# Two-layer mixer and expert model on one core: residual gain in half rows, last two tiles combined by TensorE in both layers

## The chip, the cores and the metric

One core of a Trainium2 chip runs the whole program. The metric is the device time of one execution in microseconds (us), median of three. The engines are named as the profile names them: PE is TensorE (matmuls), DVE VectorE, ACT ScalarE, POOL GpSimd, SP SyncE, which issues most DMAs.

## What is computed

512 tokens of width 1024 pass through two layers and then a second block (a gated delta rule beside a linear recurrence, and an MLP). Of the two layers, cut to what matters here:

```python
for l in range(2):
    p = x @ w_in[l]                                   # input projection
    heads = concat(_mla(p...), _mlstm(p...), _ssd(p...))
    mix = heads @ w_out[l]                            # out projection
    x = layernorm(sqrt2 * x + mix, ln1_g[l], ln1_b[l])
    ffn = hier_moe(x, ...)                            # 16 experts, 2 per token, weighted sum
    x = layernorm(sqrt2 * x + ffn, ln2_g[l], ln2_b[l])
return second_block(x, ...)
```

All of it is float32. A product keeps full precision by splitting each operand into a high and a low part (fp32r) and adding three matmuls: high x high (L124), high x low (L125), low x high (L126).

## The kernel before, in words

The 512 tokens are four tiles of 128 rows (NT = 4). The program's text isn't the order that runs: a scheduler orders the instructions of each engine, and each engine then works through its own list, waiting where data isn't there. `layer(l)` holds what the change touches:

- **Out projection.** `R` holds the residual (4 tiles x 1024). In layer 1 it is the last layer's output without gain and bias, so `ln2_g` and `ln2_b` are loaded into two `Ye` tiles and applied to whole rows: L2065 (multiply) and L2066 (add), tiles 1 and 3 on POOL, 0 and 2 on DVE. Then `fin` (L2084 on) adds each 128x256 quarter of the product to `R` (L2086), which frees the product's PSUM buffer `mm`.
- **Experts.** Twenty steps of a loop run 16 experts, each in stages. `expert` gathers its rows, multiplies by the gate and up weights (`pg`, `py`), forms `ehh` (L1118), transposes it (L1123), multiplies by the down weight, copies the two halves of the result from PSUM into a `Ye` tile (ACT, L1133), and SP stores that to `Yd` in DRAM (L2124). `self.last` remembers `ehh` of the last expert.
- **Gate.** After the loop `self.gate` is `self.last`: POOL copies one element of it into the buffer of the next weight load (L219), so that SP can issue that load (`w_gates` in layer 0, `w_in` of the second block in layer 1) only when the element exists.
- **Overflow.** A branch (L2155) handles experts with too many tokens. Ahead of it SP waits for the outstanding transfers, the last store to `Yd` among them.
- **Combine.** POOL gathers, for each tile, the rows of its two experts (L2168) into two buffers (`GTl`, `G`, `GTh`, or halves of `raw`). A tile is added to `R` either by DVE, two scalar_tensor_tensor of 128x1024 (L2174, L2175), or by PE with diagonal matrices `dg` of the routing weights (L2182) and DVE adding the 512-wide halves (L2183). Before, layer 0 does all four tiles by DVE, layer 1 tiles 2 and 3 by PE.
- **Norm.** `moments` takes the mean, the squares on ACT (L483) and the inverse root in six small operations (L165, L166), in layer 0 on POOL for tiles 0 and 1. In layer 0 ACT normalises (L2189), PE transposes (L378), and `to_T` evicts the eight transposed 128x128 blocks into `GTh` with gain and bias, columns 3, 6, 7 on ACT (L393), the rest on DVE (L395). ACT casts the high parts (`actTh`), and POOL (tiles 0 to 2) or DVE (tile 3) subtracts the low parts (`actTl`, L139). The next layer's products of that tile (`mm`, 24 matmuls of 312 columns) need both.

Of the kernel before, what the change touches and what calls it, by code (L numbers as in the profile page):

```python
# [11 lines left out]
AF = mybir.ActivationFunctionType  # L12
OP = mybir.AluOpType
AX = mybir.AxisListType

P = 128
S = 512
NT = S // P
D = 1024
# [51 lines left out]
class Kernel:  # L71
# [297 lines left out]
    def to_T(self, dst, src, i, gc=None, bc=None, pool=None, rs=None):  # L369


        nc = self.nc
        for g in range(KD // 4):
            p = self.ps("tr", [P, 4, P])
            for j in range(4):
                f = 4 * g + j
                if rs is None:
                    nc.tensor.transpose(p[:, j, :], src[:, f * P:(f + 1) * P], self.ident)  # L378
                else:
                    nc.tensor.matmul(p[:, j, :], src[:, f * P:(f + 1) * P], rs, start=True, stop=True)  # L380
            d = dst[:, 4 * g:4 * g + 4, i * P:(i + 1) * P]
            if gc is None:
                self.split(d, p)
                continue
            y = None if bc is None else self.t(pool, "GTh", [P, KD, P], bufs=2)[:, 0:4]
            for j in range(4):
                f = 4 * g + j
                if bc is None:
                    nc.scalar.activation(d.h[:, j], p[:, j], AF.Copy, scale=gc[:, f:f + 1])
                    nc.vector.scalar_tensor_tensor(d.l[:, j], p[:, j], gc[:, f:f + 1], d.h[:, j], op0=OP.mult,  # L390
                                                   op1=OP.subtract)
                elif f in (3, 6, 7):
                    nc.scalar.activation(y[:, j], p[:, j], AF.Identity, scale=gc[:, f:f + 1], bias=bc[:, f:f + 1])  # L393
                else:
                    nc.vector.tensor_scalar(y[:, j], p[:, j], gc[:, f:f + 1], bc[:, f:f + 1], op0=OP.mult, op1=OP.add)  # L395
            if bc is not None:
                self.split(d, y, "act", "pool" if i < 3 else "dve")


    def proj_tok(self, xT, key, ncols, evac, kd=KD, ks=None):  # L400
# [691 lines left out]
    def expert(self, pool, parts, idx, store, n=CAP):  # L1092


        nc, v = self.nc, self.nc.vector
        G = self.t(pool, "G", [P, D], bufs=4)
        self.rows.append(G)
        nc.gpsimd.indirect_dma_start(out=G[:n], out_offset=None, in_=self.Xd,  # L1098
                                     in_offset=bass.IndirectOffsetOnAxis(ap=idx[:n], axis=0))
        yield  # L1100
        GT = self.hl(pool, "GT", [P, KD, P], bufs=2)[:, :, 0:n]
        for g in range(2):
            p = self.ps("tr", [P, 4, n])
            for j in range(4):
                nc.tensor.transpose(p[:, j, :], G[:n, 4 * g + j:D:KD], self.ident[:n, :n])
            self.split(GT[:, 4 * g:4 * g + 4, :], p)
        yield
        self.turn = not self.turn
        pg = self.ps("pg" if self.turn else "py", [n, 512])
        for q in range(2):  # L1110
            with parts[q] as w:
                for k in range(KD):
                    self.mm(pg[:, q * 256:(q + 1) * 256], GT[:, k, :], w[k], start=k == 0, stop=k == KD - 1)
        th = self.t(pool, "eth", [P, 256], bufs=2)[:n]
        nc.scalar.activation(th, pg[:, 0:256], AF.Tanh, scale=0.5)
        v.scalar_tensor_tensor(th, th, 1.0, pg[:, 0:256], op0=OP.add, op1=OP.mult)
        hh = self.t(pool, "ehh", [P, 2, P], bufs=2)[:n]
        v.scalar_tensor_tensor(hh.rearrange("t f p -> t p f"), th.rearrange("t (p f) -> t p f", f=2), 0.5,  # L1118
                               pg[:, 256:512].rearrange("t (p f) -> t p f", f=2), op0=OP.mult, op1=OP.mult)
        self.last = hh[:, 0, :]  # L1120
        pt = self.ps("ht", [P, 2, n])
        for f in range(2):
            nc.tensor.transpose(pt[:, f, :], hh[:, f, :], self.ident[:n, :n])  # L1123
        hT = self.hl(pool, "hT", [P, 2, P], bufs=2)[:, :, 0:n]
        self.split(hT, pt)
        yield
        Y = self.t(pool, "Ye", [P, D], bufs=2)[:n]
        with parts[2] as w:
            for z in range(2):
                py = self.ps("mm", [n, 512])  # L1130
                for f in range(2):
                    self.mm(py, hT[:, f, :], w[f][:, z * 512:(z + 1) * 512], start=f == 0, stop=f == 1)
                nc.scalar.copy(Y[:, z * 512:(z + 1) * 512], py)  # L1133
        store(Y)
        yield
# [911 lines left out]
    def layer(self, l):  # L2047
# [4 lines left out]
        with ExitStack() as c:  # L2052
# [5 lines left out]
            if l:  # L2058

                gb = [self.t(mo, "Ye", [P, D], bufs=2) for _ in range(2)]  # L2060
                for t, n in zip(gb, ("ln2_g", "ln2_b")):
                    self.bcast_load(t, a[n][l - 1], D)
                for i in (1, 0, 2, 3):
                    e = nc.gpsimd if i % 2 else v
                    e.tensor_tensor(R[:, i], R[:, i], gb[0], op=OP.mult)  # L2065
                    e.tensor_tensor(R[:, i], R[:, i], gb[1], op=OP.add)  # L2066

            halves = lambda: self.t(mo, "raw", [P, 2 * UNIT]).rearrange("p (z d) -> p z d", z=2)
            gb = halves()
# [13 lines left out]

            def fin(i, q, p):  # L2084
                r = R[:, i, q * 256:(q + 1) * 256]
                v.scalar_tensor_tensor(r, r, 2 ** 0.5, p, op0=OP.mult, op1=OP.add, accum_out=sums[:, i, q:q + 1])  # L2086
                if q == 1 and i == 0:
                    self.router_fold(mo, rw, bias, gc)
                if q < 3:
                    return  # L2090
                xt = self.t(mo, "Ye", [P, D], bufs=2)
                for g in range(2):
                    p = self.ps("tr", [P, 4 * P])
                    for j in range(4):
                        f = 4 * g + j
                        nc.tensor.transpose(p[:, j * P:(j + 1) * P], R[:, i, f * P:(f + 1) * P], self.ident)
                    (nc.vector.tensor_copy if g else nc.scalar.copy)(xt[:, g * 512:(g + 1) * 512], p)
                r = R[:, i]
                nm, rs = self.moments(mo, r, sums[:, i], self.t(mo, "G", [P, D], bufs=4), 1e-5)
                u = self.t(mo, "G", [P, D], bufs=4)  # L2100
                v.scalar_tensor_tensor(u, r, nm, gb[0], op0=OP.add, op1=OP.mult)
                for k in range(KD):
                    nc.tensor.matmul(pl[:, i, :], xt[:, k * P:(k + 1) * P], rw[:, k], start=k == 0, stop=k == KD - 1)
                v.scalar_tensor_tensor(LG[:, i], pl[:, i], rs, bias, op0=OP.mult, op1=OP.add)
                v.scalar_tensor_tensor(r, u, rs, gb[1], op0=OP.mult, op1=OP.add)
                self.dump(f"x1_{l}", r, i)
                nc.sync.dma_start(self.Xd[tok(i), :], r)
# [10 lines left out]
            n = nc.values_load(cnt[0:1, 0:1], min_val=0, max_val=S)  # L2118

            ex = {}  # L2120
            if l:

                dg = self.t(mo, "dg", [P, 2, NT, P])
            store = lambda e: lambda y: nc.sync.dma_start(self.Yd[e * CAP:e * CAP + CAP, :], y)  # L2124
            for s in range(16 + 4):
                if s == 8 and l == 0:
# [2 lines left out]
                    self.pat = [("act", "dve")]  # L2129
                if s == 1:  # L2130
                    self.params(l + 1)
                if l and 4 <= s < 12:
                    j, i = divmod(s - 4, NT)
                    nc.scalar.activation(dg[:, j, i], self.ident, AF.Copy, scale=wts[j][:, i:i + 1])

                if s < 16:
                    idx = self.slot_ids(mo, PM[:, s, :], 0, "idx")
# [23 lines left out]
            Yg = [self.t(mo, tag, [P, D], bufs=n) for tag, n in [("GTl", 2)] * 2 + [("G", 4)] * 4 + [("GTh", 2)] * 2 * l]  # L2161
            if l == 0:
                z = halves()
                Yg += [z[:, 0], z[:, 1]]
            Yg = [Yg[2 * i:2 * i + 2] for i in range(NT)]
            for i in range(NT):
                for j in range(2):
# [2 lines left out]
            self.gate = [Yg[3][0]] * 2  # L2170
            for i in range(NT):
                r = R[:, i]
                if l == 0 or i < 2:
                    v.scalar_tensor_tensor(r, Yg[i][0], wts[0][:, i:i + 1], r, op0=OP.mult, op1=OP.add)  # L2174
                    v.scalar_tensor_tensor(r, Yg[i][1], wts[1][:, i:i + 1], r, op0=OP.mult, op1=OP.add,  # L2175
                                           accum_out=sums[:, i, 0:1])
                else:
                    for hf in range(2):
                        py = self.ps(("pg", "py")[hf], [P, 512])
                        hs = slice(hf * 512, (hf + 1) * 512)  # L2180
                        for j in range(2):
                            nc.tensor.matmul(py, dg[:, j, i], Yg[i][j][:, hs], start=j == 0, stop=j == 1)  # L2182
                        v.scalar_tensor_tensor(r[:, hs], py, 1.0, r[:, hs], op0=OP.mult, op1=OP.add,  # L2183
                                               accum_out=sums[:, i, hf:hf + 1])
                nm, rs = self.moments(mo, r, sums[:, i, 0:1 if l == 0 or i < 2 else 2], Yg[i][0], 0.5e-5, nc.gpsimd if i < 2 and l == 0 else v)
                xh = Yg[i][1]
                if l == 0:
                    v.tensor_tensor(nm, nm, rs, op=OP.mult)
# [75 lines left out]
```

## Time and profile before

| | us |
|---|---|
| three runs | 1707.49, 1707.58, 1709.02 |
| median | 1707.58 |
| the profiled execution's own time | 1710.83 |
| its span, first to last instruction | 1709.0 |
| PE busy | 1569.1 (92%) |
| DVE / ACT / POOL busy | 1274.3 / 835.7 / 513.2 |
| mean granted TensorE clock | 0.956 of full |

A profile shows one execution. Rows of a timeline begin with a start time and a duration in us; in square brackets stands how long the engine was idle before, and what ended that. "x2" means two instructions in one row. Times in the text are on that time line.

### The profile page before, as it was taken

The numbers are of one execution on the slowest core, as the hardware profiler recorded it, in microseconds if no ns is written. First come the engines' busy times: TensorE is split into PE (matmuls) and PEld (weight loads), VectorE is DVE, ScalarE is ACT, GpSimd is POOL, SyncE is SP. The second block draws the span as 40 slices with busy tenths as digits, with TensorE's granted clock in tenths as the row PEclk, the third lists the DMA queues.
The fourth block names the chain that finished last, engine by engine and source line by source line (L and its number), as shares of the span: only waits on it lengthen the run. The fifth ranks groups of instructions, "written<-read, shape, count | busy, mean of one in ns | idle before, by whom it ended". The sixth has DMA issues, their size and how long they took to land. (4 is left out here: it accounts for less than half of the span.)

```text
span 1709.0 us, 29588 instructions
## 1 busy us (share of the span) xinstructions
PE 1569.1 (92%) x11563; PEld 1402.5 (82%) x11563; DVE 1274.3 (75%) x2466; ACT 835.7 (49%) x1431; POOL 513.2 (30%) x446
## 2 busy tenths in 40 slices
PE   7999999699966999998889993999799999999997
PEld 6889899699956789888879972888578998998896
DVE  6758963799957847865689976777875798777764
ACT  5444551288856544561368863455532553333331
POOL 0244422404014145334315202003521144433441
PEclk9999999799987999998989997999898999999999
DMA  5214142599945211123399964422111333333311
GB/s 189 84 40 176 33 148 77 205 356 360 404 146 211 70 51 62 36 99 120 123 350 365 374 247 172 135 89 85 39 41 61 124 124 99 99 99 99 99 62 50
DMA packets 104782, 248.02 MB, mean 145 GB/s; under 512 B 6836, under 2 KB 67640, under 8 KB 92344
## 3 DMA queue, kind: packets, MB, share of 16 engines
q1 hardware_dynamic: 98744, 225.05, 37.2%
q0 software_dynamic: 5888, 20.97, 3.8%
q8 instruction: 94, 1.54, 0.4%
q14 instruction: 56, 0.46, 0.1%
HBM read 218.21 MB, written 27.79 MB: 144 GB/s over the span
## 5 line engine op out<-in xcount | busy, mean ns | idle before, releaser
L134 ACT CAST wh<-raw 128x1024 fp32r<-128x1024 f32 (+3 forms) x371 | 373.4, 1024 | 278.5 <-PE mm L125 71.7
L139 DVE TENSOR_TENSOR wl<-raw,wh 128x1024 fp32r<-128x1024 f32 (+1 forms) x273 | 327.9, 1221 | 77.2 <-ACT wh L134 76.3
L139 POOL TENSOR_TENSOR wl<-raw,wh 128x1024 fp32r<-128x1024 f32 (+2 forms) x98 | 233.8, 2397 | 375.9 <-ACT wh L134 370.4
L124 PE MATMUL mm<-wh,actTh 128*128 128x256 f32 (+2 forms) x640 | 192.3, 301 | 17.9 <-ACT wh L134 8.1
L126 PE MATMUL mm<-wh,actTl 128*128 128x256 f32 (+2 forms) x640 | 187.7, 295 | 3.0 <-POOL actTl L139 2.0
L125 PE MATMUL mm<-wl,actTh 128*128 128x256 f32 (+2 forms) x640 | 188.1, 295 | 0.5 <-DVE wl L139 0.5
L124 PE MATMUL mm<-actTh,wh 128*128 128x512 f32 x368 | 150.5, 409 | 1.7 <-DVE BA L1385 0.9
L125 PE MATMUL mm<-actTl,wh 128*128 128x512 f32 x368 | 147.6, 401 | 0.0
L126 PE MATMUL mm<-actTh,wl 128*128 128x512 f32 x368 | 147.1, 400 | 0.0
L124 PEld LDWEIGHTS mm<-wh,actTh 128*128 128x128 f32 x640 | 126.7, 198 | 22.0 <-ACT wh L134 8.1
L126 PEld LDWEIGHTS mm<-wh,actTl 128*128 128x128 f32 x640 | 125.6, 197 | 5.7 <-POOL actTl L139 3.0
L125 PEld LDWEIGHTS mm<-wl,actTh 128*128 128x128 f32 x640 | 126.6, 198 | 1.8 <-DVE wl L139 0.9
L1098 POOL DMA_INDIRECT G<-Xd,idx x32 | 70.9, 2216 | 135.4 <-DVE oh L1147 58.2
L125 PE MATMUL dn<-wl,uTh 128*128 128x512 f32 x256 | 100.6, 393 | 1.7 <-POOL wl L139 1.7
L124 PE MATMUL dn<-wh,uTh 128*128 128x512 f32 x256 | 100.7, 394 | 1.0 <-DVE R L1865 1.0
L126 PE MATMUL dn<-wh,uTl 128*128 128x512 f32 x256 | 100.1, 391 | 0.0
L124 PEld LDWEIGHTS mm<-actTh,wh 128*128 128x128 f32 x368 | 69.7, 189 | 17.9 <-PE mm L126 2.2
L126 PEld LDWEIGHTS mm<-actTh,wl 128*128 128x128 f32 x368 | 69.8, 190 | 15.7
L125 PEld LDWEIGHTS mm<-actTl,wh 128*128 128x128 f32 x368 | 69.8, 190 | 14.2
L124 PE MATMUL py<-wh,GTh 128*96 128x256 f32 x256 | 73.9, 289 | 1.3 <-ACT wh L134 1.3
L125 PE MATMUL py<-wl,GTh 128*96 128x256 f32 x256 | 73.4, 287 | 1.1 <-DVE wl L139 1.1
L124 PE MATMUL pg<-wh,GTh 128*96 128x256 f32 x256 | 74.3, 290 | 0.0
(822 smaller groups left out, 4290.6 us busy)
## 6 DMA issues: line engine op xcount, KB each, us to landing
raw<-in_expert_w_gate_dram SPq DMA_DIRECT2D x32, 1024.0 KB, 13.6
raw<-in_expert_w_up_dram SPq DMA_DIRECT2D x32, 1024.0 KB, 10.9
raw<-in_expert_w_down_dram SPq DMA_DIRECT2D x32, 1024.0 KB, 13.4
raw<-in_w_ff_dram SPq DMA_DIRECT2D x32, 1024.0 KB, 5.5
raw<-in_w_in_dram SPq DMA_DIRECT2D x27, 1024.0 KB, 4.9
raw<-in_w_out_dram SPq DMA_DIRECT2D x12, 1024.0 KB, 5.0
Yd<-Ye SPq DMA_DIRECT2D x32, 384.0 KB, 6.1
Yd<-zr SPq DMA_DIRECT2D x9, 512.0 KB, 6.6
```

Of the source, the lines that this page charges most:

```text
L124: mm(out, lhsT.h, rhs.h, start=start, stop=False, **kw)
L125: mm(out, lhsT.h, rhs.l, start=False, stop=False, **kw)
L126: mm(out, lhsT.l, rhs.h, start=False, stop=stop, **kw)
L134: nc.scalar.copy(dst.h, src)
L139: (nc.gpsimd if leng == "pool" else nc.vector).tensor_tensor(dst.l, src, dst.h, op=OP.subtract)
L1098: nc.gpsimd.indirect_dma_start(out=G[:n], out_offset=None, in_=self.Xd, in_offset=bass.IndirectOffsetOnAxis(ap=idx[:n], axis=0))
```

## The change

It has six edits, all in `to_T`, `expert` and `layer`:

```diff
 # to_T, layer 0 only (bc is not None)
-                elif f in (3, 6, 7):
+                elif f in (1, 3, 5, 7):
                     nc.scalar.activation(y[:, j], p[:, j], AF.Identity, ...)
...
-                self.split(d, y, "act", "pool" if i < 3 else "dve")
+                self.split(d, y, "act")
 # expert
-        self.last = hh[:, 0, :]
...
-        Y = self.t(pool, "Ye", [P, D], bufs=2)[:n]
+        Y = self.last = self.t(pool, "Ye", [P, D], bufs=2)[:n]
 # layer: residual of layer 1
-                for i in (1, 0, 2, 3):
-                    e = nc.gpsimd if i % 2 else v
-                    e.tensor_tensor(R[:, i], R[:, i], gb[0], op=OP.mult)
-                    e.tensor_tensor(R[:, i], R[:, i], gb[1], op=OP.add)
+                gb2 = gb
...
             def fin(i, q, p):
                 r = R[:, i, q * 256:(q + 1) * 256]
+                if l and q < 2:
+                    hs = slice(q * 512, (q + 1) * 512)
+                    v.tensor_tensor(R[:, i, hs], R[:, i, hs], gb2[0][:, hs], op=OP.mult)
+                    v.tensor_tensor(R[:, i, hs], R[:, i, hs], gb2[1][:, hs], op=OP.add)
 # layer: diagonals, now in both layers, for tiles 2 and 3 only
-            if l:
-                dg = self.t(mo, "dg", [P, 2, NT, P])
+            dg = self.t(mo, "dg", [P, 2, 2, P])
...
-                if l and 4 <= s < 12:
-                    j, i = divmod(s - 4, NT)
-                    nc.scalar.activation(dg[:, j, i], ..., scale=wts[j][:, i:i + 1])
+                if 8 <= s < 12:
+                    j, i = divmod(s - 8, 2)
+                    nc.scalar.activation(dg[:, j, i], ..., scale=wts[j][:, i + 2:i + 3])
 # layer: combine
             if l == 0:
                 z = halves()
-                Yg += [z[:, 0], z[:, 1]]
+                Yg = [z[:, 0], z[:, 1]] + Yg
...
-                if l == 0 or i < 2:
+                if i < 2:
...
-                nm, rs = self.moments(..., nc.gpsimd if i < 2 and l == 0 else v)
+                nm, rs = self.moments(...)
```

In layer 0 the buffers of the gathered rows thus change tiles: the halves of `raw` are now tile 0's, `GTl` tile 1's, `G` those of tiles 2 and 3. The scheduler then orders the engines' lists anew. Three places show it. Line numbers of the changed kernel differ by one in part (L2065/L2066 have become L2085/L2086, `fin`'s add L2086 is L2087, the copies L1133 are L1132).

**ACT, end of layer 0's experts**, before (`hTh` belongs to the last expert, `wh` 936 and 624 wide to `w_gates`):

```order
L134 CAST wh<-raw 128x1024 x2
L1133 COPY Ye<-mm 96x512
L1115 ACTIVATE eth<-py 96x256
L1133 COPY Ye<-mm 96x512 x2
L134 CAST hTh<-ht 128x2x96
L1133 COPY Ye<-mm 96x512
L134 CAST wh<-raw 128x936 x2
L1133 COPY Ye<-mm 96x512
L134 CAST wh<-raw 128x624
```

and now:

```order
L134 CAST wh<-raw 128x1024 x2
L1132 COPY Ye<-mm 96x512
L1115 ACTIVATE eth<-py 96x256
L1132 COPY Ye<-mm 96x512 x2
L134 CAST hTh<-ht 128x2x96
L1132 COPY Ye<-mm 96x512 x2
L134 CAST wh<-raw 128x936 x2
L134 CAST wh<-raw 128x624
```

The copy of the second half of the last `Ye` stood behind the two 936-wide casts; now both copies stand ahead of them. Layer 1 moves in the same way, with casts of 792 columns.

**PE, behind the overflow branch of layer 0**, before (`tr` are the transposes, `mm` the next layer's products):

```order
L2155 UNCONDITIONAL_BRANCH
L378 MATMUL tr<-ident,GTl 128x128 x8
L378 MATMUL tr<-ident,G 128x128 x4
L124 MATMUL mm<-wh,actTh 128x312
L125 MATMUL mm<-wl,actTh 128x312
L378 MATMUL tr<-ident,G 128x128 x4
L126 MATMUL mm<-wh,actTl 128x312
L124 MATMUL mm<-wh,actTh 128x312
L125 MATMUL mm<-wl,actTh 128x312
L126 MATMUL mm<-wh,actTl 128x312
```

and now:

```order
L2155 UNCONDITIONAL_BRANCH
L2182 MATMUL pg<-G,dg 128x512
L2182 MATMUL py<-G,dg 128x512
L2182 MATMUL pg<-G,dg 128x512
L2182 MATMUL py<-G,dg 128x512
L378 MATMUL tr<-ident,raw 128x128 x8
L2182 MATMUL pg<-G,dg 128x512 x2
L2182 MATMUL py<-G,dg 128x512 x2
L378 MATMUL tr<-ident,GTl 128x128 x8
L124 MATMUL mm<-wh,actTh 128x312
L125 MATMUL mm<-wl,actTh 128x312
L126 MATMUL mm<-wh,actTl 128x312
```

The combine of tile 2 stands ahead of tile 0's transposes, that of tile 3 ahead of tile 1's, and the products begin behind tile 1's transposes, in one piece of 24 for a tile.

**DVE, out projection of layer 1**, before (`Ye` are gain and bias, `eth` and `rw` the router's weights):

```order
L139 TENSOR_TENSOR actTl<-tr,actTh 128x512
L2065 TENSOR_TENSOR R<-R,Ye 128x1024 x2
L2066 TENSOR_TENSOR R<-R,Ye 128x1024 x2
L2086 SCALAR_TENSOR_TENSOR R,sums<-R,mm 128x256
L1084 TENSOR_TENSOR eth<-rw,rg 128x160
L1086 TENSOR_REDUCE rs_9680<-eth 128x20
L1084 TENSOR_TENSOR rw<-rw,rg 128x160
L1086 TENSOR_REDUCE rs_9684<-rw 128x20
L2086 SCALAR_TENSOR_TENSOR R,sums<-R,mm 128x256 x2
```

and now:

```order
L139 TENSOR_TENSOR actTl<-tr,actTh 128x512
L2085 TENSOR_TENSOR R<-R,Ye 128x512 x8
L2086 TENSOR_TENSOR R<-R,Ye 128x512 x7
L1084 TENSOR_TENSOR eth<-rw,rg 128x160
L2086 TENSOR_TENSOR R<-R,Ye 128x512
L2087 SCALAR_TENSOR_TENSOR R,sums<-R,mm 128x256 x2
L1086 TENSOR_REDUCE rs_9703<-eth 128x20
L1084 TENSOR_TENSOR rw<-rw,rg 128x160
L1086 TENSOR_REDUCE rs_9707<-rw 128x20
L2087 SCALAR_TENSOR_TENSOR R,sums<-R,mm 128x256 x3
```

All sixteen half-row operations have come to stand in one block ahead of the first add of a product, and POOL has none.

## Rows read from the trace of the kernel before

**Rows 1.** Timeline, end of layer 0's experts, SP, ACT and POOL.

```profile
493.89 0.83 SPq L225 DMA_DIRECT2D raw<-in_w_gates_dram  x2
...
495.51 6.41 SPq L2124 DMA_DIRECT2D Yd<-Ye  x2
...
497.93 0.58 ACT L1133 COPY Ye<-mm 96x512 f32<-96x512 f32 x1 [2.23 <-issue]
...
499.25 1.84 ACT L134 CAST wh<-raw 128x936 fp32r<-128x936 f32 x2 [0.73 <-DMA raw<-in_w_gates_dram]
...
505.81 1.00 POOL L2168 DMA_INDIRECT raw<-Yd,row  x1 [11.76 <-SPq L2155]
```

**Rows 2.** Windows of 2 us there: length, busy of five engines, PEclk, DMA share, GB/s.

```profile
498.00:500.00 2.00, 0.78 (x4) 0.25 (x2) 0.00 (x0) 1.27 (x2) 0.00 (x0) 1.00 0.86 297
...
500.00:502.00 2.00, 0.00 (x0) 0.00 (x0) 1.75 (x2) 2.00 (x4) 0.00 (x0) 1.00 0.16 59
```

**Rows 3.** Timeline, tail of layer 0, ACT and PE.

```profile
529.30 0.81 ACT L393 ACTIVATE GTh<-tr,par 128x128 f32<-128x128 f32 x2
...
525.00 1.97 PE L378 MATMUL tr<-ident,GTl 128*128 128x128 f32 x8 [26.23 <-ACT GTl L2189]
...
532.27 0.46 PE L124 MATMUL mm<-wh,actTh 128*128 128x312 f32 x1
...
533.05 0.46 PE L124 MATMUL mm<-wh,actTh 128*128 128x312 f32 x1
...
544.28 0.30 PE L124 MATMUL mm<-wh,actTh 128*128 128x312 f32 x1
...
544.71 0.31 PE L124 MATMUL mm<-wh,actTh 128*128 128x312 f32 x1
```

**Rows 4.** Window of the same tail, columns as in rows 2.

```profile
523.70:546.00 22.30, 19.03 (x117) 18.58 (x118) 17.25 (x59) 18.51 (x36) 12.74 (x20) 0.77 0.54 189
```

**Rows 5.** Tile actTl, 484 to 560: count, ns min/median/max, first and last start.

```profile
L126 PE MATMUL mm<-wh,actTl x32: 303/305/609, 531.1 to 547.6; 128*128 128x312 f32 x32
...
L139 POOL TENSOR_TENSOR actTl<-GTh,actTh x6: 1283/1290/1294, 529.5 to 540.4; 128x512 fp32r<-128x512 f32 x6
...
L139 DVE TENSOR_TENSOR actTl<-GTh,actTh x2: 681/686/692, 543.0 to 544.6; 128x512 fp32r<-128x512 f32 x2
```

**Rows 6.** Timeline: out projection of layer 1, DVE and PE; last, a 128x512 pair elsewhere.

```profile
783.89 4.54 DVE L2065 TENSOR_TENSOR R<-R,Ye 128x1024 f32<-128x1024 f32 x2 [1.30 <-DMA Ye<-in_ln_g_dram]
...
794.94 0.41 DVE L2086 SCALAR_TENSOR_TENSOR R<-R,mm 128x256 f32<-128x256 f32 x1
...
795.41 0.58 PE L124 MATMUL mm<-wh,actTh 128*128 128x256 f32 x1 [5.81 <-DVE R L2086]
...
614.63 1.28 DVE L890 TENSOR_TENSOR St<-St,tr 128x512 f32<-128x512 f32 x2 [3.89 <-PE tr L887]
```

**Rows 7.** Tile Ye, 760 to 800, layer 1's residual on DVE, columns as in rows 5.

```profile
L2065 DVE TENSOR_TENSOR R<-R,Ye x2: 1227/2312/3397, 783.9 to 785.0; 128x1024 f32<-128x1024 f32 x2
```

**Rows 8.** Timeline, end of layer 1's experts and its combine, SP, POOL and PE.

```profile
1021.44 0.98 SPq L229 DMA_DIRECT2D raw<-in_w_in_dram  x2
...
1022.90 7.57 SPq L2124 DMA_DIRECT2D Yd<-Ye  x2
...
1035.11 0.98 POOL L2168 DMA_INDIRECT GTl<-Yd,row  x1 [13.52 <-SPq L2155]
...
1046.38 2.04 PE L2182 MATMUL pg<-G,dg 128*128 128x512 f32 x2 [20.22 <-DMA G<-Yd,row]
...
1049.65 1.02 PE L2182 MATMUL pg<-G,dg 128*128 128x512 f32 x2
```

**Rows 9.** DMA issues at 1029.5 to 1030.5: KB each, us from issue to landing.

```profile
Yd<-Ye SPq DMA_DIRECT2D x1, 384.0 KB, 3.7
```

**Rows 10.** Windows, late experts of layer 1, columns as in rows 2.

```profile
1002.40:1005.00 2.60, 0.98 (x7) 0.73 (x7) 2.60 (x3) 2.60 (x4) 0.00 (x0) 1.00 0.00 0
...
1005.00:1008.40 3.40, 3.40 (x19) 3.40 (x18) 3.40 (x6) 2.31 (x5) 0.00 (x0) 0.50 0.37 106
```

More of the change, by code (lines that the diff above doesn't have):

```diff
@@ L2131, in layer @@
                     self.params(l + 1)
-                if l and 4 <= s < 12:
-                    j, i = divmod(s - 4, NT)
-                    nc.scalar.activation(dg[:, j, i], self.ident, AF.Copy, scale=wts[j][:, i:i + 1])
+                if 8 <= s < 12:
+                    j, i = divmod(s - 8, 2)
+                    nc.scalar.activation(dg[:, j, i], self.ident, AF.Copy, scale=wts[j][:, i + 2:i + 3])
                 if s < 16:
@@ L2181, in layer @@
                         for j in range(2):
-                            nc.tensor.matmul(py, dg[:, j, i], Yg[i][j][:, hs], start=j == 0, stop=j == 1)
+                            nc.tensor.matmul(py, dg[:, j, i - 2], Yg[i][j][:, hs], start=j == 0, stop=j == 1)
                         v.scalar_tensor_tensor(r[:, hs], py, 1.0, r[:, hs], op0=OP.mult, op1=OP.add,
                                                accum_out=sums[:, i, hf:hf + 1])
-                nm, rs = self.moments(mo, r, sums[:, i, 0:1 if l == 0 or i < 2 else 2], Yg[i][0], 0.5e-5, nc.gpsimd if i < 2 and l == 0 else v)
+                nm, rs = self.moments(mo, r, sums[:, i, 0:1 if i < 2 else 2], Yg[i][0], 0.5e-5)
                 xh = Yg[i][1]
```

## Prediction

> **What bounds the kernel now.** The page comes first: PE is busy 92% of the span, so time can be won only where PE stands idle or runs at half clock, and a change on another engine counts only as far as it moves the first matmul behind such a gap. The timeline of PE then gives the gaps that the six edits touch: the ends of both layers' experts and the out projection of layer 1. For each the rows of the other engines show what ends the gap.
>
> At the end of layer 0 the chain is: the last copy into `Ye`, the last store, SP's wait ahead of the overflow branch, the gathers, the norm, the transposes, the products. The weights are loaded early (493.89), ACT's casts of them (499.25, 1.84 us) hold the second half's copy back, the last store goes out only at 495.51 + 6.41 = 501.9, and the first gather waits until 505.81 [rows 1]. PE stands for 26 us, until the transposes at 525.00 [rows 3]. Layer 1 has the same end at 1021 to 1035 [rows 8]. In layer 1's out projection PE waits 5.81 us for the first add, which stands behind DVE's whole-row operations [rows 6].
>
> The sum is made on the time line of the profiled execution (1710.83 us; 1.8 of it lies outside the span of 1709.0). That one was 3.25 above the median of the three runs, 1707.58. I apply the differences to the median. A difference of 0.2%, 3.4 us, is about what a measurement of this kernel can tell from no change.
>
> **A. End of layer 0: 1.1 us lost.** The gate copy now waits for `Ye` in place of `ehh`. I take it to wait for the first half only, since it reads one element: that copy ends at 497.93 + 0.58 = 498.5, POOL's copy follows, the loads go out at about 498.9, 5.0 later than before [rows 1]. In return the casts no longer stand ahead of the second copy, and the last store goes out near 499.7, 2.2 earlier, but it stands behind the loads on SP's queue. Before, the same three transfers (936 + 312 KB of weights, one store of 384 KB) took from 493.89 until the rate fell, 297 GB/s before 500 and 59 after it, so to about 500.4 [rows 1, 2]: 6.5 us. From 498.9 that makes 505.4. From landing to the first gather layer 1 needed 1035.11 - (1022.90 + 7.57 - 0.3 + 3.7) = 1.2 [rows 8, 9]. So the first gather starts at 506.6, **0.8 later** than 505.81. Bounds: 0.9 earlier, if the store isn't held (first rival); 1.4 later, if the gate waits for both halves (another 0.58).
>
> This is where a rule bears on the sum. The Trainium skill, "DMA: Bandwidth & Descriptors", section "Two DMAs through the same engine are not ordered", says that within one queue of an engine descriptors start in order, though they need not finish so. By that rule a store issued behind the loads starts behind them, and the sum stays as it is; without it the first rival holds. No row here shows a store that overtook a load.
>
> Behind the gathers the work is ordered anew. Tile 2's first buffer is the fifth, 11.3 us behind the first gather in layer 1 (1035.11 to 1046.38), and its combine took from 1046.38 until about 1051.5 [rows 8]: in layer 0 it runs from 517.9 to 523.1. Tile 0's transposes wait behind it on PE, so the earlier norm of tile 0 (roots on DVE instead of POOL) is hidden by that combine and costed at nothing; without the cover it could give at most 1 or 2 us. They end at about 524.1 (eight took 1.97 at half clock [rows 3], half of it is taken). From there ACT sets the pace. Before, it was busy 18.51 of 22.30 us in that tail [rows 4]. Now two normalisations of 128x1024 (1.25 each, an estimate from the next smaller rows) come ahead of it, and four evictions (two took 0.81 [rows 3]) join: 18.5 - 2.5 + 1.6 = 17.6. With the same 3.8 of waits its last cast ends at 545.5, and the last tile's 24 products at 0.43/3 = 0.143 (544.28 to 544.71 [rows 3]) end at 549.0. Before, they ended at 547.6 + 0.3 = 547.9 [rows 5]. So **A = +1.1**, of which 0.8 is the gathers. The low parts move from POOL (six of 1.29) to DVE (0.69 [rows 5]): 4.1 us more for DVE, which had 5.0 free in the tail [rows 4], hidden behind ACT's casts; without that cover the last tile would lose up to 1.4. Bounds of A: -0.6 to +3.5 (the gathers' 1.4 plus that 1.4 and 0.7 of smaller waits).
>
> **B. Residual in half rows, layer 1: 1.0 us gained.** Written in `fin`, a half row could be made just ahead of the add that needs it. The order doesn't have it so: all eight multiplications, seven additions, a small router operation and the last addition stand ahead of the first add. So PE's wait changes only by the block's length. Before: from 783.89 to 794.94 + 0.41 = 795.35 [rows 6], four whole-row operations, of which the second took 3.40 in place of 1.23 while POOL worked on its own two tiles [rows 7]. Now POOL has none, and DVE does sixteen of 128x512. Two in a row took 1.28 [rows 6], one alone 0.69 (as the low part of 128x512 [rows 5]), so each further one adds 0.59 or 0.60: 16 x 0.60 = 9.6, with 0.41 each for the router's operation and the add, 794.3. **B = -1.0.** Bounds: at 0.69 each +0.4, at 0.59 without the router's operation -1.5. PE's gap shrinks from 5.8 to 4.8, and its products behind it still start at half clock.
>
> **C. End of layer 1: 1.0 us gained.** The same gate and copies. The loads move 5.0 as in layer 0, from 1021.44 to 1026.4 [rows 8]; with the same 6.5 (the transfers are 12% smaller, which I leave as a margin) all has landed at 1032.9, and the first gather starts at 1034.1 in place of 1035.11, since here the last store had gone out much later (1030.2 [rows 8]) than the loads. **C = -1.0**, bounds -3.0 (store not held: 1027.2 + 3.7 + 1.2 = 1032.1) and +0.3 (gate waits for both halves, 0.6, and smaller moves). Behind it the order of the combine stays.
>
> **D. Late experts of layer 1: 0.5 us gained, open.** The scheduler has moved transposes of `ehh` and six of the down products among the up products. Before, PE was idle for 1.6 us in 1002.4 to 1005.0, and for the 3.4 us behind it had half clock [rows 10], which cost half of that, 1.7. Bounds: -3.3 if both go, +0.8 if transposes now wait for `ehh` on PE (half of the old idle time). Nothing shows that they go, so I take a small part, -0.5.
>
> **The diagonals** are four more 128x128 operations of ACT in layer 0 and four fewer in layer 1 (0.41 each as the eviction [rows 3], 1.6 us); ACT is busy half of the span, and they lie in the middle of the experts. Costed at nothing; without that cover +1.6 and -1.6.
>
> **Sum:** 1.1 - 1.0 - 1.0 - 0.5 = -1.4, so 1707.58 - 1.4 = **1706.2**, no change that can be told. Chance 0.62, own range 1703.5 to 1709.5.
>
> **Rival 1, the last store isn't held by the loads.** Then A's first gather comes at 499.7 + 0.3 + 3.7 + 1.2 = 504.9, 0.9 earlier: A = -0.9 + 0.3 = -0.6, and C = -3.0. Sum -0.6 - 1.0 - 3.0 - 0.5 = -5.1: **1702.5**. For it: a store alone landed in 3.7 us [rows 9]. Against it: the loads are issued ahead of it on the same queue, and SP waits for the loads too. Chance 0.17.
>
> **Rival 2, slower: PE keeps half clock through the products of layer 0's tail.** PE now starts with a combine, waits, transposes, waits again. A product took 0.78/3 = 0.26 at half clock (532.27 to 533.05) and 0.143 at full [rows 3], so a tile of 24 costs 2.8 us more, and its transposes 1.0. If the clock is low for the first two tiles, much of that fills PE's own waits for ACT. Tile 0's products begin at about 529 (524.1, four matmuls of tile 3's combine at up to 1.02 [rows 8], tile 1's transposes): 529 + 6.2 + 2.0 + 6.2 + 1.0 + 3.5 + 1.0 + 3.5 = 552.4, +3.4, a total of 1709.6. It decides from the third tile on: 556.1, 7.1 later than 549.0, **1713.3**. For it: PE came out of its gap at half clock before and still had it at 533.05, 8 us after its first transposes [rows 3]; the tail's mean was 0.77 [rows 4]. Against it: in layer 1 the same combine was back at full clock by 1050, 3.3 us after it began (2.04 for the first, 1.02 for the third [rows 8]). The Trainium skill, "TensorE: Matmul & The Clock Gate", section "HAM oscillation — how this bites in real kernels", describes a PE that waits for data between groups of matmuls and goes to and fro between its two rates; that would favour this rival. Chance 0.12.
>
> **Rival 3, the products do follow their half rows.** Then the gap of 5.8 and about 2 us of half clock behind it go: B = -7.8 in place of -1.0, **1699.4**. The order speaks against it. Chance 0.03. The remaining 0.06 is spread on both sides (D's bounds).
>
> **How the numbers follow.** Faster than 1704.2: rivals 1 and 3 (0.20) and the lower edge of the forecast (0.06): 0.26. Slower than 1711.0: rival 2 and a part of the rest: 0.14. Same: 0.60. The range of 8 in 10 takes in rival 1 and the bounds of A and D: 1701.5 to 1711.0; rivals 2 and 3 and the rest's edges, under 0.2, are left out.
>
> **What would show it.** First gather of layer 0 some 0.8 later behind the last expert's product, and PE's fourth tile ending about 1 us later; first gather of layer 1 a microsecond earlier; PE's gap in the out projection near 4.8, with DVE's block of halves ahead of the first add and half clock after it. Wrong, if gathers start within 4.5 us of the last `Ye` copy (rival 1), if products of 0.46 run past the second tile (rival 2), or if the gap in the out projection is gone (rival 3).

## The result and the profile after

| | before | after |
|---|---|---|
| median of five runs, us | 1707.58 | 1717.66 |
| lowest to highest | 1706.65 to 1709.02 | 1716.75 to 1718.40 |
| ratio, 95% interval | | 1.0051 [1.0038, 1.0064] |
| profiled execution's span | 1709.0 | 1716.6 |

The change makes the kernel slower by half a per cent, 8.7 us by the ratio; the interval leaves no doubt of it. In a second set of runs it was 1.0050 [1.0035, 1.0065]. The forecast was 1706.2 with a range up to 1711.0, so it was wrong, in sign and in size.

First the places that the prediction names. **End of layer 0's experts**, timeline of the changed kernel, which answers to [rows 1]; the last lines are DVE's low parts of the new weights, and its first instruction behind the overflow branch:

```profile
496.26 1.15 SPq L225 DMA_DIRECT2D raw<-in_w_gates_dram  x2
...
497.51 0.37 SPq L2124 DMA_DIRECT2D Yd<-Ye  x1
...
495.41 0.58 ACT L1132 COPY Ye<-mm 96x512 f32<-96x512 f32 x1 [2.24 <-issue]
...
496.29 0.58 ACT L1132 COPY Ye<-mm 96x512 f32<-96x512 f32 x1 [0.31 <-PE mm L126]
...
501.70 2.46 ACT L134 CAST wh<-raw 128x936 fp32r<-128x936 f32 x3 [4.83 <-DMA raw<-in_w_gates_dram]
...
506.49 0.99 POOL L2168 DMA_INDIRECT raw<-Yd,row  x1 [10.11 <-SPq L2155]
...
502.71 2.18 DVE L139 TENSOR_TENSOR wl<-raw,wh 128x936 fp32r<-128x936 f32 x2 [9.15 <-ACT wh L134]
...
507.44 0.81 DVE L139 TENSOR_TENSOR wl<-raw,wh 128x624 fp32r<-128x624 f32 x1 [2.56 <-DVEq L2155]
```

The copies now stand side by side at 495.41 and 496.29, and the last store goes out at 497.51, ahead of ACT's casts, as predicted. The first gather comes at 506.49, close to the 506.6 of the forecast, but by luck: PE's last product ended at 496.26 (498.78 before), so the way from there to the first gather is 10.2 us; it was 7.0 before (505.81 [rows 1]), and 7.8 had been forecast. The windows there, answering to [rows 2], show the transfers: they reach their highest rate (352 GB/s) only from 498 on, some 2 us after the first load's issue, and trail off until 506. The last update of the store's semaphore, which is its landing, stands in the trace at 505.30, 9.0 behind that issue; the gather follows 1.2 later, as it did before (504.62 and 505.81).

```profile
496.00:498.00 2.00, 0.26 (x2) 0.00 (x0) 0.00 (x0) 0.58 (x1) 0.33 (x2) 1.00 0.43 71
...
498.00:500.00 2.00, 0.00 (x0) 0.00 (x0) 0.00 (x0) 0.00 (x0) 0.00 (x0) 1.00 0.96 352
...
500.00:502.00 2.00, 0.00 (x0) 0.00 (x0) 0.00 (x0) 0.29 (x1) 0.00 (x0) 0.67 0.91 286
...
502.00:504.00 2.00, 0.00 (x0) 0.00 (x0) 1.29 (x2) 2.00 (x3) 0.00 (x0) 0.50 0.35 139
...
504.00:506.00 2.00, 0.00 (x0) 0.00 (x0) 0.88 (x1) 0.16 (x1) 0.00 (x0) 0.50 0.04 12
```

**Tail of layer 0**, answering to [rows 3] and [rows 5]:

```profile
518.14 2.05 PE L2182 MATMUL pg<-G,dg 128*128 128x512 f32 x2 [21.89 <-DVE R L2175]
...
523.14 1.04 PE L378 MATMUL tr<-ident,raw 128*128 128x128 f32 x8
...
528.25 0.39 PE L124 MATMUL mm<-wh,actTh 128*128 128x312 f32 x1
528.47 0.30 PE L125 MATMUL mm<-wl,actTh 128*128 128x312 f32 x1
...
533.79 1.09 PE L378 MATMUL tr<-ident,G 128*128 128x128 f32 x8 [1.86 <-ACT G L2189]
...
535.43 0.46 PE L125 MATMUL mm<-wl,actTh 128*128 128x312 f32 x1
...
540.87 1.09 PE L378 MATMUL tr<-ident,G 128*128 128x128 f32 x8 [0.61 <-ACT GTh L393]
...
L126 PE MATMUL mm<-wh,actTl x32: 302/306/629, 528.6 to 549.4; 128*128 128x312 f32 x32
```

Tile 2's combine, tile 0's transposes and the first product stand within a microsecond of the forecast (517.9, 523.1, 529). The products start at full clock (rows of 0.30 us follow the first). Then PE waits for ACT's normalisation ahead of tile 2's transposes (1.86), and the next tile's first eleven products run at half clock (0.46 in most; they start 0.30 apart on average in place of 0.143, which costs some 1.5 us). The last product ends at 549.4 + 0.3, 43.3 behind the first gather (42.1 before).

**Out projection of layer 1**, answering to [rows 6]:

```profile
785.58 4.90 DVE L2085 TENSOR_TENSOR R<-R,Ye 128x512 f32<-128x512 f32 x8 [1.15 <-DMA Ye<-in_ln_g_dram]
...
790.40 4.29 DVE L2086 TENSOR_TENSOR R<-R,Ye 128x512 f32<-128x512 f32 x7
...
794.62 0.31 DVE L1084 TENSOR_TENSOR eth<-rw,rg 128x160 f32<-128x160 f32 x1
...
794.86 0.68 DVE L2086 TENSOR_TENSOR R<-R,Ye 128x512 f32<-128x512 f32 x1
...
795.46 0.41 DVE L2087 SCALAR_TENSOR_TENSOR R<-R,mm 128x256 f32<-128x256 f32 x1
...
795.93 0.58 PE L124 MATMUL mm<-wh,actTh 128*128 128x256 f32 x1 [4.73 <-DVE R L2087]
```

All sixteen half rows run ahead of the first add, as the order said, at 0.61 us each. From landing of `Ye` to the end of the first add it takes 10.3 us in place of 11.5, and PE's gap is 4.73 in place of 5.81.

**End of layer 1's experts**, answering to [rows 8] and [rows 9] (the last line is the DMA view of the last store, KB and us from issue to landing):

```profile
1029.46 0.98 SPq L229 DMA_DIRECT2D raw<-in_w_in_dram  x2
...
1030.54 0.41 SPq L2124 DMA_DIRECT2D Yd<-Ye  x1
...
1035.23 2.14 ACT L134 CAST wh<-raw 128x792 fp32r<-128x792 f32 x3 [5.16 <-SPq L2155]
...
1036.11 1.88 DVE L139 TENSOR_TENSOR wl<-raw,wh 128x792 fp32r<-128x792 f32 x2 [9.34 <-ACT wh L134]
...
1040.56 0.71 DVE L139 TENSOR_TENSOR wl<-raw,wh 128x528 fp32r<-128x528 f32 x1 [2.57 <-DVEq L2155]
...
1041.05 1.08 POOL L2168 DMA_INDIRECT GTl<-Yd,row  x1 [11.46 <-DVEq L2155]
...
Yd<-Ye SPq DMA_DIRECT2D x1, 384.0 KB, 7.1
```

The store lands 7.1 us after its issue, where a store alone took 3.7 [rows 9]. DVE ends the low parts of the new weights at 1037.99, and its next instruction, behind the branch, begins 2.57 later. POOL's first gather is released by DVE's passage of the branch, and starts at 1041.05: 11.6 us after the last product, 8.9 before, and 3.4 after the store's landing, where it was 1.2.

### The profile page after: what moved, and what is told of

The parts are those of the page before. It is cut to its first block, busy times and chain, and to the rows that moved or that the text cites. A ratio compares the mean times of both kernels' runs of the same rounds, so it can differ in the third digit from the quotient of the medians.

```text
span 1716.6 us, 29622 instructions
## 1 busy us (share of the span) xinstructions
PE 1576.3 (92%) x11579; PEld 1403.3 (82%) x11579; DVE 1271.9 (74%) x2496; ACT 836.4 (49%) x1435; POOL 480.7 (28%) x424
## 5 line engine op out<-in xcount | busy, mean ns | idle before, releaser
L125 PE MATMUL mm<-actTl,wh 128*128 128x512 f32 x368 | 147.6, 401 | 0.0
L125 PE MATMUL pg<-wl,GTh 128*96 128x256 f32 x256 | 73.7, 288 | 0.3 <-DVE wl L139 0.3
```

The costliest lines, as they stand in the source:

```text
L125: mm(out, lhsT.h, rhs.l, start=False, stop=False, **kw)
```

## The experiments

Every run's profile was cut at the same events. The numbers are differences between starts or ends of rows of its timeline, in us. "Branch" is the end of the last expert product to the first gather, "tail" the first gather to the end of layer 0's last tile's product, "rows" the landing of `Ye` to the end of the first add, "second block" the opening of the last gate copy (L219) to the end of the span. Ratios are to runs of the kernel before on the same chip, with 95% intervals. Single runs of one kernel spread by some 10 us there, so one profile's total says little and the ratios are the verdict. The expectations of experiments 1 to 4 count the branch from the start of the last product, 0.4 us earlier than the table does.

| run | branch 0 | tail 0 | rows | branch 1 | second block | ratio |
|---|---|---|---|---|---|---|
| before | 7.0 | 42.1 | 11.5 | 8.9 | 641.0 | 1 |
| the change | 10.2 | 43.3 | 10.3 | 11.6 | 641.8 | 1.0051 [1.0038, 1.0064] |
| the change again | 9.9 | 44.8 | 10.3 | 11.5 | 642.0 | 1.0050 [1.0035, 1.0065] |
| 1 change, gate back | 7.4 | 44.6 | 10.3 | 8.3 | 638.3 | 1.0004 [0.9987, 1.0021] |
| 2 gate alone | 9.8 | 42.8 | 11.5 | 9.5 | 636.9 | 1.0010 [0.9996, 1.0025] |
| 3 half rows alone | 7.0 | 41.8 | 10.3 | 8.9 | 638.5 | 0.9976 [0.9961, 0.9991] |
| 4 combine alone | 7.2 | 43.2 | 11.5 | 8.8 | 642.2 | 1.0025 [1.0011, 1.0039] |
| 5 store on another queue | 7.9 | 44.2 | 11.5 | 9.4 | 636.9 | 1.0010 [1.0000, 1.0020] |
| 6 half rows, loads behind branch | 4.5 | 45.1 | 10.3 | 5.1 | 636.8 | 0.9976 [0.9962, 0.9990] |
| 7 half rows, no gate | 4.9 | 40.7 | 10.3 | 4.9 | 635.4 | 0.9939 [0.9927, 0.9952] |
| 7 again | 5.2 | 41.8 | 10.3 | 4.8 | 634.8 | 0.9923 [0.9909, 0.9938] |
| 8 change, no gate | 5.3 | 43.1 | 10.3 | 4.8 | 635.3 | 0.9939 [0.9926, 0.9953] |
| 9 gate and half rows | 10.1 | 42.1 | 10.3 | 9.4 | 638.7 | 1.0008 [0.9996, 1.0019] |

**Experiments 1 to 4: which edit.** In 1 the gate goes back to `ehh` in the changed kernel; 2 to 4 make one edit of the change in the kernel before (4: the whole combine, that is everything but gate and half rows).

```diff
 # 1, against the change; 2 is the reverse, against the kernel before
+        self.last = hh[:, 0, :]
-        Y = self.last = self.t(pool, "Ye", ...)
+        Y = self.t(pool, "Ye", ...)
 # 3, against the kernel before
-                for i in (1, 0, 2, 3):
...
+                if l and q < 2:
+                    hs = slice(q * 512, (q + 1) * 512)
+                    v.tensor_tensor(R[:, i, hs], R[:, i, hs], gb2[0][:, hs], op=OP.mult)
+                    v.tensor_tensor(R[:, i, hs], R[:, i, hs], gb2[1][:, hs], op=OP.add)
 # 4, against the kernel before
-                elif f in (3, 6, 7):
+                elif f in (1, 3, 5, 7):
...
-                self.split(d, y, "act", "pool" if i < 3 else "dve")
+                self.split(d, y, "act")
...
-                Yg += [z[:, 0], z[:, 1]]
+                Yg = [z[:, 0], z[:, 1]] + Yg
...
-                if l == 0 or i < 2:
+                if i < 2:
...
```

Expected of 1: 

> The changed kernel with one edit undone: the gate is on ehh again. Theory 1 (the late gate: the loads go out about 5 us later, so the last store behind them lands later and the casts and low parts of the new weights come to the overflow branch last): from the last expert product to the first gather, layer 0 goes back from 10.6 to about 7.4 us and layer 1 from 12.0 to about 9.3; the time falls by 5 to 7 to 1711 to 1713. Theory 2 (the tail of layer 0, where ACT sets the pace, and PE's clock are to blame): the first gathers move, but the time stays at 1715 to 1718.

Expected of 2: 

> The kernel before with the gate on Ye alone. Theory 1: from the last expert product to the first gather about 10.6 us in layer 0 and 12.0 in layer 1, in place of 7.4 and 9.3; the time is 1712 to 1715. Theory 2: within 2 us of 1707.6.

Expected of 3: 

> The kernel before with the residual in half rows alone. Theory 1 and theory 2: from the landing of Ye to the first add 10.3 us in place of 11.5, a gain of 1.2 there; the time is 1705.5 to 1707.5, if nothing behind it takes the gain away. Rival (what the products win, the first expert loses to half clock after the routing): the gain is there at the first add and gone by the first expert, 1707.5 to 1710.

Expected of 4: 

> The kernel before with the edits of layer 0's combine alone (tiles 2 and 3 by TensorE, diagonals of two tiles, roots and low parts by VectorE, four evictions on ScalarE). Theory 1: the tail from first gather to last product is about 1 us longer than before (43.2 against 42.1), the time 1708 to 1710. Theory 2: the combine carries most of the loss, 1712 to 1716.

The gate moves the branch in both layers, there and back: 7.4 and 8.3 without it, 9.8 to 10.2 and 9.5 to 11.6 with it. Undoing it in the change gives back all of the loss (1.0051 to 1.0004, some 8 us where theory 1 named 5 to 7); between the two profiles (1716.6 and 1708.3) the branches are 6.1 of it, and 3.5 come from the second block, which is the subject below. The half rows are worth 1.2 us wherever they stand; the kernel with them alone is faster by 0.24%, 4.1 us, which is more than forecast; in its profile the second block is 2.5 shorter. The combine alone is slower by 0.25%, 4.3 us, above theory 1's range and just under theory 2's; its tail is 1.1 longer, as theory 1 had it. The gate alone missed theory 1's time: the first gathers were late (9.8 as expected in layer 0; 9.5 in layer 1, less than expected), but the time was only 0.10% above, the number of theory 2. The table shows where that went: its second block is 4 us shorter, though no edit touches it.

**Experiment 9 and the second block.** The change without the combine's edits:

```diff
 # against the kernel before: half rows as in 3, and
-        self.last = hh[:, 0, :]
-        Y = self.t(pool, "Ye", ...)
+        Y = self.last = self.t(pool, "Ye", ...)
```

Expected: 

> The change without the edits to the combine: the gate on Ye and the half rows. Its second block has the order of one 128x512 square root on ScalarE, and of the VectorE operations beside it, that the runs with the short second block have (637 to 638.5 us from the last gate to the end, against 641 to 642 in the change). Theory (that order, not chance, sets the 3 to 4 us): 636 to 639. Rival (chance of the clock): 636 to 642, with no relation to the order. From the last product to the first gather 9.8 to 10.2 in layer 0 and 9.4 to 11.6 in layer 1; the ratio 0.999 to 1.002.

Both came out so (the operation named there is a tanh, L1666, not a square root): the branches are late, and the second block is 2.3 us shorter than before. In that block the scheduler puts this tanh either ahead of two small copies or behind them. ACT's order in the changed kernel, and with the gate back:

```
L1663 ACTIVATE R<-mm 128x512
L1579 ACTIVATE T_15101<-sm 32x128 x2
L1666 ACTIVATE R<-R 128x512
L1570 COPY AT<-Y_14713 32x4x32 x2
```

```
L1664 ACTIVATE R<-mm 128x512
L1580 ACTIVATE T_15101<-sm 32x128 x2
L1571 COPY AT<-Y_14713 32x4x32 x2
L1667 ACTIVATE R<-R 128x512
```

The first order stands in the kernel before, the change and experiments 4 and 6, the second in all others. From the start of this tanh to the end of the span the kernel before, the change with its repeat, and experiment 4 take 464.9 to 465.5 us, and those with the second order 460.4 to 461.8. But experiment 6 has the first order on ACT and takes 461.7: ACT's order alone does not set the length. Two pairs whose second block has the same order on PE, DVE and ACT agree within 0.2 us, though run apart: 1 and 3 (638.3, 638.5), 2 and 5 (636.9 each). Some 225 us into the block PE is at half clock behind a wait; the windows (columns as in [rows 2]) of the change, and then of experiments 1 and 6 at the same events:

```profile
1300.00:1305.00 5.00, 2.41 (x11) 1.84 (x10) 1.56 (x3) 0.62 (x1) 2.00 (x2) 0.78 0.64 209
...
1305.00:1310.00 5.00, 5.00 (x27) 4.66 (x26) 2.65 (x7) 0.63 (x1) 0.00 (x0) 0.50 0.30 97
...
1310.00:1315.00 5.00, 5.00 (x34) 5.00 (x33) 2.22 (x12) 0.00 (x0) 0.00 (x0) 0.70 0.00 0
```

```profile
1295.00:1300.00 5.00, 3.51 (x14) 2.92 (x15) 0.62 (x2) 0.62 (x1) 1.27 (x1) 0.50 0.62 212
...
1300.00:1305.00 5.00, 5.00 (x42) 4.81 (x42) 3.70 (x12) 0.63 (x1) 0.00 (x0) 0.90 0.09 30
...
1305.00:1310.00 5.00, 5.00 (x45) 4.76 (x44) 4.15 (x17) 0.00 (x0) 0.00 (x0) 1.00 0.00 0
```

```profile
1295.00:1300.00 5.00, 5.00 (x39) 4.81 (x39) 3.19 (x9) 0.63 (x1) 0.00 (x0) 0.83 0.21 70
1300.00:1305.00 5.00, 5.00 (x46) 5.00 (x45) 4.26 (x20) 0.00 (x0) 0.00 (x0) 1.00 0.01 2
```

In the change PE works 12.4 us of 15, with 0.50 of the clock in the second window and 0.70 in the third; in experiment 1 it is back at 0.90 and 1.00, and in experiment 6 at 0.83 and 1.00. The length goes with PE's clock in this stretch. Experiment 6 has the order of experiment 4 on PE and ACT there, but not on DVE; what brings the clock back sooner was not tried, so the cause of the second block's length stays open.

**Experiment 5: queue or branch?** Against experiment 2, only the last store changes its queue:

```diff
-store = lambda e: lambda y: nc.sync.dma_start(...)
+store = lambda e: lambda y: (nc.scalar if e == 15 else nc.sync).dma_start(...)
```

Expected: 

> The gate on Ye alone, and only the last expert's store issued on ScalarE's queue, so that it does not stand behind the loads. Theory 1a (the store held on the queue): last product to first gather falls from 9.8 to about 7.5 us in layer 0 and from 9.5 to about 7.5 in layer 1. Theory 1b (casts and low parts of the new weights ahead of the branch, and SP's wait for the loads): it stays at 9 to 10 in both.

POOL's first two gathers of layer 0 in experiment 5, where PE's last product ends at 497.51; then the end of layer 1's experts, where it ends at 1030.65, with the store's landing:

```profile
505.44 1.60 POOL L2167 DMA_INDIRECT raw<-Yd,row  x1 [7.79 <-DVE wl L139]
509.16 1.14 POOL L2167 DMA_INDIRECT GTl<-Yd,row  x1 [2.13 <-DVEq L2154]
```

```profile
1037.40 1.88 DVE L139 TENSOR_TENSOR wl<-raw,wh 128x792 fp32r<-128x792 f32 x2 [9.44 <-ACT wh L134]
...
1039.71 0.71 DVE L139 TENSOR_TENSOR wl<-raw,wh 128x528 fp32r<-128x528 f32 x1 [0.44 <-ACTq L2154]
...
1040.10 1.18 POOL L2167 DMA_INDIRECT GTl<-Yd,row  x1 [9.32 <-SPq L2154]
...
Yd<-Ye ACTq DMA_DIRECT2D x1, 384.0 KB, 7.2
```

In layer 0 the first gather falls from 9.8 to 7.9, by most of what 1a asked for, but it comes alone: the second is released by DVE's passage of the branch and starts 11.7 behind the last product, as late as in experiment 2 (11.8). In layer 1 the branch stays at 9.4 (1b). The store lands 7.2 us after its issue on ACT's queue, no sooner than behind the loads on SP's (6.7 in experiments 2 and 9, 7.1 in the change). The low parts of the new weights end at 1037.40 + 1.88 = 1039.28, and the first gather follows 0.8 later, as it does in experiments 2 and 9, while its distance from the store's landing differs (1.6 to 1.8). POOL's row names SP, which passes the branch last by a little. So another queue for the store gains nothing: the ratio is 1.0010 in both.

**Experiments 6 and 7: neither in the way.** Both are experiment 3 with the call that starts the loads, casts and low parts put behind the branch in the text. In 6 a gate on tile 1's second gather holds them there; in 7 nothing does, and the scheduler lifts them ahead of the branch, among the last experts.

```diff
-            self.gate = [self.last] * 2
-            self.set_phase("m", [self.raw0], [self.ring0], [("act", "dve")])
...
             with tc.If(n > CAP):
                 self.overflow(l, mo, PM, raw1, ring2)
             x2.close()
             x1.close()
 # 7: here
+            self.gate = []
+            self.set_phase("m", [self.raw0], [self.ring0], [("act", "dve")])
...
 # 6: behind the gathers instead
+            self.gate = [Yg[1][1]] * 2
+            self.set_phase("m", [self.raw0], [self.ring0], [("act", "dve")])
```

Expected of 6: 

> Half rows alone, and the next layer's first loads, casts and low parts moved behind the overflow branch, gated on the gather of tile 1. Theory 1 (the store behind the loads, and casts and low parts ahead of the branch, hold the gathers): with neither, the store lands 3.0 to 3.7 us after its issue and the first gather comes 5.5 to 6.5 us after the last product in both layers (before 7.0 and 8.9); the weights are then ready about 20 us after the first gather and the first products (24 after it) need not wait; ratio 0.994 to 0.997. Rival (the weights come too late for the products of tile 0): the products begin 2 to 4 us later behind the gathers; ratio 0.998 to 1.001.

Expected of 7: 

> Half rows alone, and the next layer's first loads with no gate at all: the scheduler puts them among the last experts. Theory 1a (what counts is when the loads and the last store have landed): from the last expert product to the first gather 6 to 7 us in layer 0 and 6 to 8 in layer 1 (before 7.0 and 8.9); ratio 0.996 to 0.998. Rival (the loads take bandwidth from the last experts' weights): the gathers come sooner behind the last product, but that product comes 2 to 4 us later; ratio 0.998 to 1.001.

The same stretch of the timeline in experiment 7, where PE's last product ends at 1022.21:

```profile
1020.09 3.07 SPq L2126 DMA_DIRECT2D Yd<-Ye  x2
...
1019.45 0.71 DVE L139 TENSOR_TENSOR wl<-raw,wh 128x528 fp32r<-128x528 f32 x1 [0.22 <-ACT wh L134]
...
1022.25 0.58 ACT L1133 COPY Ye<-mm 96x512 f32<-96x512 f32 x1 [0.76 <-PE mm L126]
...
1027.07 0.95 POOL L2170 DMA_INDIRECT GTl<-Yd,row  x1 [68.69 <-SPq L2155]
```

In both, the branch takes 4.5 to 5.2 us in either layer: less than the forecast of 5.5 and more. In 6 that is given back, as its rival had it: the ratio is that of experiment 3. The weights come too late, layer 0's tail is 45.1, and layer 1's way from the first gather to the next gate is 37.8 (33.1 in experiment 3). In 7 it stays. The rival, that the loads slow the last experts, is not borne out: the way from the first expert's transposes to the last product is 146.9 us in layer 0 and 146.6 in layer 1 (146.8 and 146.7 before). Experiment 7 beats both kernels, by 0.61% and again by 0.77%. Of the 12.3 between its span (1696.7) and that of before, the branches are 6.1, the half rows 1.2 and the tail 1.4; the second block adds 5.6, whose cause is not shown, and the rest goes the other way. So the ratio is not the branches' gain alone.

Expected of its repeat: 

> Half rows with no gate, once more, beside the two others of this set: ratio 0.993 to 0.996, the second block's stage 635 to 637.

Expected of the change's repeat, beside 5 to 7: 

> The changed kernel again, beside the others of this set. Theory 1 (gate and layer 0's combine add up): ratio to before 1.003 to 1.006. Rival (the first comparison was partly chance, since single edits on their own gave 1.001 for the gate and 0.998 for the half rows): 1.000 to 1.003.

**Experiment 8: the combine with nothing else in play.** The change with the gate removed as in 7; its second block has the order of experiment 7 on DVE and ACT, and but for a pair of 32x32 products on PE.

Expected: 

> The whole change, but with no gate on the next layer's first loads. It has the second block in the same order as the run with half rows and no gate, so the two differ by the edits to the combine alone. Theory (the combine's edits lengthen layer 0's tail): from first gather to last product 42.5 to 44.5 us against 40.7, layer 1's tail 34 to 35; the ratio to before is 0.995 to 0.998, above 0.994 of the run without them. Rival (the combine by TensorE is no loss once the gathers start early): within 0.001 of 0.994.

The ratio came out as the rival had it, the tail as the theory had it. Between 0.9939 for this and 0.9923 for experiment 7 in the same set, a little under its forecast, the intervals overlap, so the ratios don't decide; the medians (1699.93 and 1696.92) and the tail (43.1 against 40.7 and 41.8) point to a loss of 1 to 3 us, as experiment 4 does.

## Why the prediction was wrong, by its own steps

**A, forecast 1.1 us lost: the step from the loads to the first gather failed.** The shift of the loads came true, and the store went out ahead of the casts, as forecast. "Until the rate fell" was then taken for landing: 6.5 us from the first load's issue. But the rate shows when bytes move, not when a transfer counts as landed: before, the last of the same three transfers landed at 501.42 in the trace, 7.5 after the first load's issue and 1.0 after the fall of the rate; in the change it took 9.0 (496.26 to 505.30) in layer 0 and 8.2 (1029.46 to 1030.54 + 7.1) in layer 1. The 1.2 from landing to gather held in layer 0. Measured: 3.2 later behind the last product in place of 0.8. Why the landing took 1.5 longer than before is not shown. The tail was put 0.3 longer and is 1.2 to 2.7 longer. PE does wait for ACT (1.86), as said, but the half clock that followed this wait in the change, some 1.5, had no term; in the repeat, by the trace, the clock was full from 523.5 on, and its longer tail is not explained.

**C, forecast 1.0 gained: the same step, and a wait that was left out.** The 1.2 us from landing to gather were read where SP comes to the branch last. The casts and low parts of the loaded weights stand ahead of the branch on ACT and DVE, and with late loads these come last: DVE's low parts, its passage of the branch, then POOL. The text counted what the casts no longer held back (the copy), and not what they themselves hold: the branch. Measured: 2.7 later. Experiments 2 and 9, with the same late loads, come to 9.5 and 9.4, 0.5 to 0.6 later than before; the other 2.1 are DVE's slow passage of the branch in the change, whose cause is open (last section).

**The rule weighed at A** (the Trainium skill, "DMA: Bandwidth & Descriptors", section "Two DMAs through the same engine are not ordered": within one queue of a DMA engine descriptors start in order) is not contradicted, but the queue's order isn't what made the store late in layer 1: there it landed 7.1 after its issue behind the loads and 7.2 on another queue, in place of 3.7 alone. What else delayed it was not tried apart.

**B, forecast 1.0 gained: right,** 1.2 in each of the seven kernels with half rows, by the mechanism forecast: a shorter block, not an interleaved one.

**D, forecast 0.5 gained: not borne out.** From the first expert's transposes of `ehh` to the last product layer 1 took 147.6 and 149.2 us in the change, 146.7 before, and 145.5 in experiment 9, which has the gate too. The half clock that D wanted shorter had only moved: before it stood at 1005.0 to 1008.4 [rows 10], in the change the granted clock is 1.00 at the same events and 0.66 in 1015 to 1020. By the trace there is one such stretch in the change, there are two in its repeat and none in experiment 9; what places them is not shown.

**The diagonals** at nothing: no run isolates them. Layer 0's experts took 146.8 us with the combine alone (experiment 4), as before.

**What had no term** is the second block, which the prediction held to be untouched because the diff doesn't reach it. The scheduler reorders it, and it is up to 7 us longer or shorter between variants. In the change it stays as before (641.8), so it explains little of the loss; but each kernel that has the gate and a shorter second block looks nearly harmless in its total. An estimate from the table takes the second block's difference off each ratio: the gate alone then costs 5.8 us, the combine 3.1, the half rows give 1.6, together 7.3 lost, against 7.9 for the change. Each ratio is good to some 2.5 us.

**The rivals.** The first (store not held) fell with the gathers; the second (half clock in layer 0's tail) in the main, since the products began at full clock and were at half clock again only for part of the second tile; the third as the order said. None had the branch as the place where late weights cost.

Together, in the two profiles: branches +3.2 and +2.7, tail +1.2, half rows -1.2, which is +5.9 of the 7.6 between the spans; the rest lies in stretches of some 2 us either way (layer 0's experts came 2.5 sooner, layer 1's began 1.9 later behind the first add, where the granted clock of 866 to 874 was 0.58 in place of 0.85). With the gate undone the ratio is 1.0004 [0.9987, 1.0021], with a second block that helps.

## What to carry to other kernels

Work for a later stage that stands ahead of a branch on any engine's list can hold what stands behind the branch on another's. Here POOL's gathers waited for the store's landing, which SP waits for, and for DVE's passage, behind low parts that nobody needed yet; with neither in the way they came 2 to 4 us sooner than before. It is not a full barrier: in layer 0 of experiment 5 one gather started (505.44) while DVE was still at work ahead of the branch, and only the next waited. Prefetch for the next stage belongs well ahead of such a branch or, if it isn't needed soon, behind it, and a gate that makes a prefetch later should be priced by the last engine to reach the branch. Under a scheduler compare stages and not totals alone, since a small edit can reorder, and move, code that it never names.

## What had not been expected of the hardware

- DVE's first instruction behind the branch began 2.57 us after its last one ahead of it in layer 1 of the change (1037.99 to 1040.56), and 2.40 in its repeat, but 0.33 in experiments 2 and 9 and 0.43 in 5 with the same instructions around it; in layer 0 it is 2.5 to 2.7 in all of these. That is why layer 1's branch is 11.5 in the change and 9.4 there. The cause stays open.
- A transfer can count as landed a while after most of its bytes have moved: in layer 0 of the change the rate was down to 12 GB/s in 504 to 506, and the store's landing stands at 505.30; in layer 1 the rate was 20 GB/s in 1036 to 1037 and 8 in 1037 to 1038, and the store's landing stands at 1037.6.
- A store on a queue of its own landed as late as one behind the loads: 7.2 us after its issue in layer 1 of experiment 5, 6.7 to 7.1 on the loads' queue, 3.1 to 3.7 alone.
